# Decay factors of the gated delta rule from broadcast rows of cumulated sums, and two gate tiles moved from the plain to the block product

## The chip, the cores and the metric

The kernel runs on one core of a Trainium2 chip. The metric is the device time of one execution in microseconds (us), the median over several executions. The engines are TensorE (PE in the profile, its weight loads PEld), VectorE (DVE), ScalarE (ACT), GpSimd (POOL) and SyncE (SP), each with an instruction queue of its own that is worked off in order.

## What is computed

One decoder layer on 1024 tokens of width 1024: an input projection, two token mixers side by side (a gated delta rule with 8 heads of 128, and latent attention), their merge through sigmoid gates, a layer norm, a feed-forward block and a second layer norm. The change touches the delta rule's preparation and the gates' projection. For each head, with chunks of tokens, the reference does this:

```python
g = jnp.cumsum(g, axis=-1)                                # log decays, summed within the chunk
diff = g[..., :, None] - g[..., None, :]
decay = jnp.where(tril, jnp.exp(jnp.where(tril, diff, 0.0)), 0.0)
l_mat = jnp.where(strict, jnp.einsum('bnhid,bnhjd->bnhij', k_beta, k) * decay, 0.0)
intra = jnp.where(tril, jnp.einsum('bnhid,bnhjd->bnhij', q, k) * decay, 0.0)
q_dec = q * jnp.exp(g)[..., None]
...
o_dn = rms_norm(o_dn, dn_norm_w[i]) * jax.nn.silu(z)      # z: 8 of the 24 gate tiles
mixed = jax.nn.sigmoid(gate_dn) * y_dn + jax.nn.sigmoid(gate_mla) * y_mla   # the other 16
```

The kernel works with chunks of 128 tokens, so a head has 8 of them.

## The kernel before

All products are made of two parts for each operand, a high and a low one: `split` casts the high part on ACT (line 63) and subtracts it from the source for the low part on DVE (line 64). Three matmuls (high-high, high-low, low-high) stand for each fp32 product.

The projection `x @ w_in` has 24 tiles of 128 columns for q, k, v (with a short convolution behind each) and 24 gate tiles (8 for z, 16 for the two gates). They are worked off in two ways. A **plain gate tile** (`gate_tile`, line 155) is 8 x 3 x 2 = 48 matmuls of 128x128 by 128x512 into two of the four PSUM banks A to D; three gate tiles run at the very start in another form, and with `NG0 = 6` the tiles 3, 4 and 5 are plain ones. A **pair** (`pair`, line 479) takes two tiles at once and forms their 2x2 block product with 7 products in place of 8, of 12 matmuls each (line 501), so 84 matmuls for two tiles. Four of the 7 products need sums of x quarters: T1, T2, T3 and T4, which DVE (lines 450, 451) and POOL (452, 453) form after the early phase out of a second load of x (line 445, tiles `c0` to `c3`, tags for each of the four rows of blocks k), and which are then split as well. The ACT half of these splits is kept behind the last activation of gate tile 3 on ACT (`issue_after(g3.ins)`). The first pair's matmuls are kept behind the last transposes of `rope_q` on PE. The products of all pairs use the banks A, B, C, D in turn, so a product can begin when the one four before it has been read. The first two pairs (`first`) do their three products with plain quarters of x first, then T2, T1, T3, T4.

The pairs stand in a list: four blocks of three convolution pairs and some gate pairs, by `NGB = (1, 1, 2, 5)`. That is 12 + 9 = 21 pairs. After the third pair of a block, four **units** of `dn_unit` become due (two heads, two halves of the sequence), and one of them is issued behind each of the next pairs; there are 16.

A unit loads q, k and v of a head and 512 tokens, transposes them (line 587 for k and q, 604 for v, PSUM tag `t` with two buffers), and forms the decays: 8 small scaled copies of a triangular mask on ACT (568), two fp32r matmuls with `m_gt_r` (572) and one bf16 matmul that adds -1e30 above the diagonal (573), an Exp out of PSUM into `dm` (575), two fp32r matmuls with ones (578) and an Exp out of PSUM into `er` (580). Then POOL multiplies `er` by k and q (609), PE forms k.k and k.q (616, PSUM tag `s` with two buffers, which the two decay results use too), and DVE scales these by `dm` (619).

The order of instructions on each engine is set by a planner that simulates a timeline when the program is built; the program text gives only dependences and hints.

Of the kernel before, what the change touches and what calls it, by code (L numbers as in the profile page):

```python
# [7 lines left out]
F32 = mybir.dt.float32  # L8
F32R = mybir.dt.float32r
BF16 = mybir.dt.bfloat16  # L10
I32 = mybir.dt.int32
AF = mybir.ActivationFunctionType
ALU = mybir.AluOpType
# [4 lines left out]
P = 128  # L18
S = 1024
D = 1024  # L20
NT = S // P
KT = D // P
H = 8
# [13 lines left out]
def tile_hybrid_block(ctx: ExitStack, tc: tile.TileContext, A: dict):  # L37
    nc = tc.nc
# [23 lines left out]
    def split(src, hi, lo):  # L62
        nc.scalar.copy(hi, src)  # L63
        nc.vector.tensor_tensor(lo, src, hi.bitcast(F32), ALU.subtract)  # L64

    dram = pool(ctx, "dram", space=DRAM)
# [6 lines left out]
    n_d = dram.tile([P, 64, 64], F32, name="n_d")  # L73
    u_d = dram.tile([P, 64, 64], F32, name="u_d")
    v11_d = dram.tile([64, 64, 64], F32, name="v11_d")
    z_d = dram.tile([H, P, S], F32, name="z_d")
    gdn_d = dram.tile([KT, P, S], F32, name="gdn_d")
    gml_d = dram.tile([KT, P, S], F32, name="gml_d")
# [16 lines left out]
    nhalf = high.tile([P, 4], F32, name="nhalf", padded_shape=[P, 56])  # L95
    const = pool(ctx, "const")
    masks = const.tile([P, 4, P], F32, name="masks")
    ident, m_gt, m_le, m_neg = (masks[:, i] for i in range(4))
    m_gt_r = const.tile([P, P], F32R, name="m_gt_r")
    ident_b = const.tile([P, P], BF16, name="ident_b")  # L100
    neg_b = const.tile([P, P], BF16, name="neg_b")
    ones = const.tile([P, P], F32, name="ones")
    nc.vector.memset(ones, 1.0)
    ones_r = const.tile([P, P], F32R, name="ones_r")
    nc.scalar.copy(ones_r, ones)
    half = const.tile([P, 64], F32, name="half")
    nc.vector.memset(half, 0.5)
    nc.vector.memset(nhalf, -0.5)
# [3 lines left out]
    sk = const.tile([P, H, NT], F32, name="sk")  # L112
    ck = const.tile([P, H, NT], F32, name="ck")
    beta = const.tile([P, NT, H], F32, name="beta")
    eg = const.tile([P, NT, H], F32, name="eg")
    egd = const.tile([P, NT, H], F32, name="egd")
    egl = const.tile([P, NT, H], F32, name="egl")
    g_hl = const.tile([P, 2, NT, H], F32R, name="g_hl")

    xs = ExitStack()  # L120
    xp = pool(xs, "xp", side="right")
# [13 lines left out]
    def s_tile(tag="s"):  # L135
        return psf.tile([P, 512], F32, name=tag, bufs=2)
# [36 lines left out]
    pp = pool(p1, "p1")  # L173
# [8 lines left out]
    for k in range(KT):  # L182
# [12 lines left out]
            nc.sync.dma_start(out=xst[:, ns], in_=A["xT"][:, k, ns])  # L195
        if k == 2:
            nc.scalar.dma_start(out=masks, in_=A["masks"])
            nc.scalar.copy(m_gt_r, m_gt)
            nc.vector.tensor_copy(ident_b, ident)
            nc.vector.tensor_copy(neg_b, m_neg)  # L200
            nc.scalar.dma_start(out=cw, in_=A["conv_w"])
            nc.scalar.dma_start(out=dnw, in_=A["dn_norm_w"])
# [7 lines left out]
        for m in range(NF):  # L210
            for j, (a, b) in enumerate(HL):
                for n in range(2):
                    nc.tensor.matmul(fps[m][n], fw[m][k // 4][a][:, k % 4], xT[b][k][n],
                                     start=(k == 0 and j == 0), stop=(k == KT - 1 and j == 2))
    NG0 = 6


    def lat_w(off, wd):
# [100 lines left out]
    def side():  # L319
# [18 lines left out]
        for hf in range(2):  # L338
            tp = s_tile("t").rearrange("p (t a) -> p t a", t=4)
# [26 lines left out]
        nc.scalar.activation(nea, alog[:, 0], AF.Exp)  # L366
        g = pp.tile([P, NT, H], F32, name="g")
        nc.vector.scalar_tensor_tensor(g, acc, -1.0, nea.unsqueeze(1).broadcast_to([P, NT, H]), op0=ALU.mult, op1=ALU.mult)
        split(g, g_hl[:, 0], g_hl[:, 1])
        yield  # L370
        yield
        gc = s_tile()[:, 0:P].rearrange("p (a t h) -> p a t h", a=2, t=NT)
        nc.tensor.matmul(gc[:, 0], m_le, g, start=True, stop=True)
        nc.tensor.matmul(gc[:, 1], ones, g, start=True, stop=True)
        nc.scalar.activation(eg, gc[:, 0], AF.Exp)
        nc.scalar.activation(egl, gc[:, 1], AF.Exp)
        gcs = pp.tile([P, NT, H], F32, name="gcs")
        nc.vector.tensor_copy(gcs, gc[:, 0])
        nc.vector.tensor_tensor(gcs, gc[:, 1], gcs, ALU.subtract)
        nc.scalar.activation(egd, gcs, AF.Exp)  # L380


    def rope_q(t, cq):
# [42 lines left out]
    def r_tile(tag, shape, dt=F32):  # L426
        return rp_.tile(shape, dt, name=tag, bufs=1)
# [131 lines left out]
    def dn_unit(h, hf):  # L559
        t0, ns = hf * 4, slice(hf * 512, (hf + 1) * 512)  # L560
# [1 line left out]
        kq = r_tile("c0", [P, 2, 512]) if hf == 0 else g2.tile([P, 2, 512], F32, name="kq", bufs=1)  # L562
        nc.sync.dma_start(out=kq[:, 0], in_=qkv_d[1][h][:, ns])
        nc.sync.dma_start(out=kq[:, 1], in_=qkv_d[0][h][:, ns])
        gm = r_tile("c2", [P, 2, 4, P], F32R)
        for i in range(2):
            for t in range(4):
                nc.scalar.activation(gm[:, i, t], m_le, AF.Copy, scale=g_hl[:, i, t0 + t, h:h + 1].bitcast(F32))

        dps = s_tile().rearrange("p (t a) -> p t a", t=4)  # L570
        for i in range(2):
            nc.tensor.matmul(dps, m_gt_r, gm[:, i], start=i == 0, stop=False)
        nc.tensor.matmul(dps, neg_b, ident_b.unsqueeze(1).broadcast_to([P, 4, P]), start=False, stop=True)
        dm = r_tile("e4", [P, 4, P])
        nc.scalar.activation(dm, dps, AF.Exp)
        eps_ = s_tile().rearrange("p (t a) -> p t a", t=4)
        for i in range(2):
            nc.tensor.matmul(eps_, ones_r, gm[:, i], start=i == 0, stop=i == 1)
        er = r_tile("e5", [P, 4, P])
        nc.scalar.activation(er, eps_, AF.Exp)  # L580
        vT = r_tile("e0", [P, 512])
        nc.sync.dma_start(out=vT, in_=qkv_d[2][h][:, ns])
        ktok, vp = r_tile("e1", [P, 4, P]), r_tile("e2", [P, 4, P])
        for which in (0, 1):
            tp = s_tile("t").rearrange("p (t a) -> p t a", t=4)
# [16 lines left out]
        tp = s_tile("t").rearrange("p (t a) -> p t a", t=4)  # L602
# [24 lines left out]

    gates = [(24 + m, 24 + m + 1) for m in range(NG0, 24, 2)]
    dn_units = []
    NGB = (1, 1, 2, 5)  # L630
    order = []
    for b, ng in enumerate(NGB):
        h = 2 * b
# [516 lines left out]
    for t in range(NT):  # L1150
# [13 lines left out]
        for hf in range(2):  # L1164
            tp = s_tile("t").rearrange("p (h a) -> p h a", h=4)
# [51 lines left out]
    for q in range(4):  # L1217
# [7 lines left out]
        for t in range(NT):  # L1225
            tq = slice(t % 4 * P, (t % 4 + 1) * P)
            ps = s_tile()[:, 0:256]
            for k in range(KT):
                for j, (a, b) in enumerate(HL):
                    nc.tensor.matmul(ps, mT[a][k // 4, t // 4][:, k % 4, tq], wg[k][b], start=(k == 0 and j == 0),  # L1230
                                     stop=(k == KT - 1 and j == 2))
# [362 lines left out]
```

## Time and profile before

| | |
|---|---|
| time, three executions | 2102.81 us, 3379.37 us, 2095.53 us (median 2102.81) |
| the profiled execution | 2099.7 us, of which 2096.8 us from the first to the last instruction |
| TensorE clock granted, mean | 0.991 of full speed |
| busy share of the span | PE 97%, DVE 67%, ACT 45%, POOL 31% |

The execution that the profile was taken from lies between the two ordinary times of the table. A busy PE in the profile is one with a matmul under way; matmuls overlap, so a row's time is longer than the step from one matmul's start to the next.

### The profile page before, as it was taken

How to read it: one execution, taken by the hardware profiler on the slowest of the kernel's cores; microseconds unless marked ns; L12 is line 12 of the kernel's file. 1: busy time of each engine (PE TensorE's matmuls, PEld its weight loads, DVE VectorE, ACT ScalarE, POOL GpSimd, SP SyncE). 2: the span in 40 equal slices, each digit the busy share in tenths (PEclk: the TensorE clock that was granted, in tenths of full speed). 3: DMA queues.
4: the chain of work that ended last, by engine and by line, in shares of the span. 5: the costliest groups of instructions: out<-in, count | busy, mean ns of one | idle time of the engine just before them, and what ended most of it. 6: DMA issues, size and time to landing. Idle time of an engine off the chain costs nothing. (4 is left out here: it accounts for less than half of the span.)

```text
span 2096.8 us, 29713 instructions
## 1 busy us (share of the span) xinstructions
PE 2030.8 (97%) x10438; PEld 1710.7 (82%) x10438; DVE 1400.7 (67%) x2169; ACT 947.8 (45%) x1938; POOL 651.8 (31%) x567
## 2 busy tenths in 40 slices
PE   8999999999999999998999999999999999999998
PEld 7887887878787888787788788899888888887876
DVE  5548887877665655543556466487888788775576
ACT  5335576677574555444334233233333333343233
POOL 0115353434343998931111000100111121111942
PEclk9999999999999999999999999999999999999999
DMA  6344366555467212137977675025434344168773
GB/s 222 114 161 151 128 194 191 184 187 169 149 203 271 73 65 68 52 111 235 282 246 242 224 241 187 26 96 200 132 115 138 130 143 133 71 208 277 271 232 112
DMA packets 232661, 347.72 MB, mean 166 GB/s; under 512 B 44800, under 2 KB 123584, under 8 KB 231744
## 3 DMA queue, kind: packets, MB, share of 16 engines
q1 hardware_dynamic: 213184, 316.45, 46.0%
q10 hardware_dynamic: 15648, 13.65, 2.1%
q0 software_dynamic: 3680, 15.73, 2.1%
q8 instruction: 82, 1.34, 0.3%
q14 instruction: 67, 0.55, 0.1%
HBM read 228.01 MB, written 117.74 MB: 165 GB/s over the span
## 5 line engine op out<-in xcount | busy, mean ns | idle before, releaser
L1460 PE MATMUL f<-wh,xh 128*128 128x512 f32 x792 | 183.7, 392 | 5.5 <-ACT xh L63 3.7
L1460 PEld LDWEIGHTS f<-wh,xh 128*128 128x128 f32 x792 | 149.2, 189 | 39.2 <-ACT xh L63 4.5
L63 ACT CAST w<-S 128x512 fp32r<-128x512 f32 x172 | 106.1, 618 | 137.5 <-PE D L1273 42.8
L1372 POOL TENSOR_TENSOR T<-act 128x512 f32<-128x512 f32 x22 | 32.2, 1463 | 398.2 <-issue 138.8
L64 DVE TENSOR_TENSOR w<-S,w 128x512 fp32r<-128x512 f32 x172 | 136.1, 791 | 9.9 <-ACT w L63 9.7
L1273 PE MATMUL A<-m,w 128*128 128x512 f32 x504 | 121.2, 389 | 0.0
L1273 PEld LDWEIGHTS A<-m,w 128*128 128x128 f32 x504 | 94.5, 188 | 19.6
L827 POOL TENSOR_TENSOR nl<-nl,itmp 128x486 f32<-128x486 f32 (+44 forms) x106 | 107.2, 1027 | 1.4
L898 PE MATMUL y<-om,w 128*128 128x512 f32 x384 | 99.4, 405 | 3.0 <-ACT w L63 2.5
L825 POOL TENSOR_TENSOR itmp<-nl 128x486 f32<-128x486 f32 (+44 forms) x106 | 93.2, 898 | 16.7 <-DMA nl<-n_d 12.2
L1113 POOL TENSOR_TENSOR lrs<-sm,nhalf 128x1 f32<-128x1 f32 x16 | 23.2, 1454 | 229.7 <-issue 135.6
L1146 PE MATMUL f<-wo,m 128*128 128x512 f32 x384 | 90.7, 392 | 0.2 <-DVE acc L1104 0.2
L63 ACT CAST w<-wst 128x512 fp32r<-128x512 f32 (+1 forms) x52 | 42.3, 816 | 106.3 <-DMA wst<-in_w_br_mla_dram 44.9
L64 DVE TENSOR_TENSOR w<-wst,w 128x512 fp32r<-128x512 f32 (+1 forms) x52 | 50.2, 967 | 59.9 <-ACT w L63 59.8
L898 PEld LDWEIGHTS y<-om,w 128*128 128x128 f32 x384 | 70.3, 191 | 18.1 <-ACT w L63 3.3
L1146 PEld LDWEIGHTS f<-wo,m 128*128 128x128 f32 x384 | 71.4, 188 | 15.1 <-DVE acc L1104 0.6
L64 DVE TENSOR_TENSOR pt<-t,pt 128x512 fp32r<-128x512 f32 (+1 forms) x96 | 52.1, 554 | 43.7 <-ACT pt L63 43.2
L763 PE MATMUL o<-pt,vv 128*128 128x512 f32 (+3 forms) x288 | 76.3, 367 | 3.6 <-ACT pt L63 1.4
L743 DVE TENSOR_REDUCE row<-f 128x1 f32<-128x128 f32 (+3 forms) x64 | 48.2, 753 | 41.0 <-PE f L741 40.4
L549 DVE SCALAR_TENSOR_TENSOR c<-zo,cw,c 128x1023 f32<-128x1023 f32 (+2 forms) x42 | 61.8, 1472 | 14.4 <-ACT c L547 14.3
L1230 PE MATMUL s<-r,m 128*128 128x256 f32 x576 | 69.7, 283 | 0.0
L1230 PEld LDWEIGHTS s<-r,m 128*128 128x128 f32 x576 | 69.4, 192 | 0.1
(490 smaller groups left out, 5349.6 us busy)
## 6 DMA issues: line engine op xcount, KB each, us to landing
acc<-in_w_ffn_in_dram SPq DMA_DIRECT2D x44, 512.0 KB, 4.0
xs_d<-xo SPq DMA_DIRECT2D x88, 256.0 KB, 2.5
xh<-xs_d SPq DMA_DIRECT2D x88, 256.0 KB, 3.5
wst<-in_w_main_dram SPq DMA_DIRECT2D x25, 512.0 KB, 4.4
a<-in_w_ffn_out_dram SPq DMA_DIRECT2D x44, 256.0 KB, 5.2
raw<-in_w_main_dram SPq DMA_DIRECT2D x20, 512.0 KB, 4.5
xs<-xf_d SPq DMA_DIRECT2D x33, 256.0 KB, 3.5
wst<-in_w_br_mla_dram SPq DMA_DIRECT2D x16, 512.0 KB, 4.5
```

The source lines that it names most:

```text
L63: nc.scalar.copy(hi, src)
L64: nc.vector.tensor_tensor(lo, src, hi.bitcast(F32), ALU.subtract)
L549: nc.vector.scalar_tensor_tensor(acc[:, d:], v[:, 0:S - d], cw[:, m, 3 - d:4 - d], acc[:, d:], op0=ALU.mult, op1=ALU.add)
L743: nc.vector.tensor_reduce(nm, ps[:, 0:nk], axis=AX.X, op=ALU.max, negate=True)
L763: nc.tensor.matmul(po[:, i0 * P:512], vv[kt][a][:, hh * P:(hh + 1) * P], hl[b][:, 0:w], start=(kt == 0 and j == 0), stop=(kt == last and j ...
L825: nc.gpsimd.tensor_tensor(tv, nl[:, k0:kn_, k:k + 1].broadcast_to([P, kn_ - k0, w]), nl[:, k:k + 1, k + 1:64].broadcast_to([P, kn_ - k0, w ...
L827: nc.gpsimd.tensor_tensor(nl[:, k0:kn_, k + 1:64], nl[:, k0:kn_, k + 1:64], tv, ALU.subtract)
L898: nc.tensor.matmul(ps, w[a][:, k], od[b][:, k, ns] if dn else om[k][b], start=(k == 0 and j == 0), stop=(k == KT - 1 and j == 2))
L1146: nc.tensor.matmul(ps[:, ns], mT[a][kh, t // 4][:, k % 4, t % 4 * P:(t % 4 + 1) * P], wo[k][b][:, ns], start=(k == 0 and j == 0), stop=(k ...
L1230: nc.tensor.matmul(ps, mT[a][k // 4, t // 4][:, k % 4, tq], wg[k][b], start=(k == 0 and j == 0), stop=(k == KT - 1 and j == 2))
L1273: nc.tensor.matmul(bank, w[a][:, k], x[b][:, k], start=(k == 0 and j == 0), stop=(k == 3 and j == 2))
L1460: nc.tensor.matmul(bk, x[a][:, t * P:(t + 1) * P], w[b], start=(k == 0 and j == 0), stop=(k == HH - 1 and j == 2))
```

## The change

Each unit no longer forms its decays on PE. `side` (early, once) now transposes the cumulated sums and writes them to DRAM as rows (`gc_d`, one row of 128 for each head and chunk) and keeps their negative per token (`ngc`). A unit loads four rows, spread over all 128 partitions, into `gr[:, 0]`; POOL adds the mask `m_up` (-1e30 where a decay must vanish, 0 elsewhere) into `gr[:, 1]`; four Exp with the per-partition bias `ngc` give `dm`, and one Exp of `gr[:, 0]` gives `er`. The five matmuls and the eight small copies go. And `NG0` falls from 6 to 4, with one gate pair more in the second block: plain are the first three tiles and tile 3, and the list of pairs has 22 entries.

```diff
@@ side()
-        split(g, g_hl[:, 0], g_hl[:, 1])
...
-        nc.scalar.activation(eg, gc[:, 0], AF.Exp)
         nc.scalar.activation(egl, gc[:, 1], AF.Exp)
-        gcs = pp.tile([P, NT, H], F32, name="gcs")
-        nc.vector.tensor_copy(gcs, gc[:, 0])
-        nc.vector.tensor_tensor(gcs, gc[:, 1], gcs, ALU.subtract)
-        nc.scalar.activation(egd, gcs, AF.Exp)
+        gcs = pp.tile([P, H, NT], F32, name="gcs")
+        nc.vector.tensor_copy(gcs, gc[:, 0].rearrange("p t h -> p h t"))
+        nc.vector.tensor_scalar(ngc, gc[:, 0], -1.0, None, op0=ALU.mult)
+        gl = pp.tile([P, NT, H], F32, name="gl")
+        nc.vector.tensor_tensor(gl, gc[:, 1], ngc, ALU.add)
+        nc.scalar.activation(egd, gl, AF.Exp)
+
+        tp = s_tile("t")
+        nc.tensor.transpose(tp[0:H * NT, 0:P], gcs.rearrange("p h t -> p (h t)"), ident)
+        gr = pp.tile([P, P], F32, name="gr")
+        nc.scalar.copy(gr[0:H * NT], tp[0:H * NT, 0:P])
+        nc.scalar.dma_start(out=gc_d, in_=gr[0:H * NT])
@@ dn_unit()
-        gm = r_tile("c2", [P, 2, 4, P], F32R)
-        for i in range(2):
-            for t in range(4):
-                nc.scalar.activation(gm[:, i, t], m_le, AF.Copy, scale=g_hl[:, i, t0 + t, h:h + 1].bitcast(F32))
-
-        dps = s_tile().rearrange("p (t a) -> p t a", t=4)
-        for i in range(2):
-            nc.tensor.matmul(dps, m_gt_r, gm[:, i], start=i == 0, stop=False)
-        nc.tensor.matmul(dps, neg_b, ident_b.unsqueeze(1).broadcast_to([P, 4, P]), start=False, stop=True)
+        gr = r_tile("c2", [P, 2, 4, P])
+        nc.sync.dma_start(out=gr[:, 0].rearrange("p t a -> p (t a)"),
+                          in_=gc_d[h * NT + t0:h * NT + t0 + 4].rearrange("i p -> (i p)").partition_broadcast(P))
+
+        nc.gpsimd.tensor_tensor(gr[:, 1], gr[:, 0], m_up.unsqueeze(1).broadcast_to([P, 4, P]), ALU.add)
         dm = r_tile("e4", [P, 4, P])
-        nc.scalar.activation(dm, dps, AF.Exp)
-        eps_ = s_tile().rearrange("p (t a) -> p t a", t=4)
-        for i in range(2):
-            nc.tensor.matmul(eps_, ones_r, gm[:, i], start=i == 0, stop=i == 1)
+        for t in range(4):
+            nc.scalar.activation(dm[:, t], gr[:, 1, t], AF.Exp, bias=ngc[:, t0 + t, h:h + 1])
         er = r_tile("e5", [P, 4, P])
-        nc.scalar.activation(er, eps_, AF.Exp)
+        nc.scalar.activation(er, gr[:, 0], AF.Exp)
@@ lists
-    NG0 = 6
+    NG0 = 4
-    NGB = (1, 1, 2, 5)
+    NGB = (1, 2, 2, 5)
```

## Rows read from the trace of the kernel before

**Rows 1.** Page, part 1: busy time, share of the span, instructions of each engine.
```profile
PE 2030.8 (97%) x10438; PEld 1710.7 (82%) x10438; DVE 1400.7 (67%) x2169; ACT 947.8 (45%) x1938; POOL 651.8 (31%) x567
```

**Rows 2.** Windows, pair by pair: length, busy time, clock granted, DMA share, GB/s.
```profile
300.98:324.30 23.32, 23.32 (x111) 19.28 (x109) 21.06 (x28) 16.58 (x34) 10.69 (x7) 1.00 0.60 182
347.62:375.27 27.65, 25.49 (x110) 20.27 (x109) 15.97 (x29) 19.02 (x37) 9.10 (x7) 0.94 0.59 185
```

**Rows 3.** Waits of 250 to 650 us: us in total, times, longest.
```profile
PE s L616 <- ACT e L580: 5.5, 3, 2.0
...
PE s L616 <- ACT e L575: 2.4, 3, 2.0
```

**Rows 4.** Timeline of PE, a unit behind a gate pair; idle before in brackets.
```profile
569.38 1.93 PE L616 MATMUL s<-c 128*128 128x256 f32 x4 [2.01 <-ACT e L575]
...
573.66 2.08 PE L616 MATMUL s<-c 128*128 128x256 f32 x4 [1.49 <-ACT e L580]
...
579.80 0.61 PE L604 MATMUL t<-masks,e 128*128 128x128 f32 x4
```

**Rows 5.** Timeline of ACT at the same unit.
```profile
567.44 1.28 ACT L575 ACT_TABLE_LOAD   x1
...
571.72 1.28 ACT L580 ACT_TABLE_LOAD   x1
...
573.51 2.14 ACT L568 ACTIVATE c<-masks,g_hl 128x128 fp32r<-128x128 f32 x7
...
576.02 0.59 ACT L591 ACTIVATE e<-t 128x512 f32<-128x512 f32 x1
```

**Rows 6.** Timeline of PE at one unit's decays: start, us, instructions.
```profile
277.66 0.61 PE L572 MATMUL s<-c,m_gt_r 128*128 128x512 f32 x2
...
278.80 1.03 PE L587 MATMUL t<-masks,kq 128*128 128x128 f32 x8
```

**Rows 7.** Window of PE alone: busy, clock granted, DMA share, GB/s.
```profile
560.00:580.00 20.00, 16.50 (x59) 0.74 0.39 131
```

**Rows 8.** DMA issues: count, KB each, us to landing.
```profile
gm<-rv_d SPq DMA_DIRECT2D x16, 256.0 KB, 5.2
```

**Rows 9.** Timeline of POOL beside the x sums.
```profile
159.47 1.29 POOL L474 TENSOR_TENSOR S<-S,wst 128x512 f32<-128x512 f32 x1
```

**Rows 10.** Timeline of PE, two products of a pair.
```profile
200.82 2.88 PE L501 MATMUL A<-xT,w 128*128 128x512 f32 x12
203.54 2.88 PE L501 MATMUL B<-xT,w 128*128 128x512 f32 x12
```

**Rows 11.** Timeline of PE where the first pair begins.
```profile
165.18 5.73 PE L161 MATMUL C<-xT,w 128*128 128x512 f32 x24 [2.17 <-ACT zo L166]
...
184.35 0.61 PE L501 MATMUL D<-T,w 128*128 128x512 f32 x2
...
190.72 0.73 PE L501 MATMUL D<-T,w 128*128 128x512 f32 x2 [0.47 <-DVE T L64]
```

**Rows 12.** Timeline of DVE: last rope split, first and last x sum.
```profile
142.60 0.69 DVE L64 TENSOR_TENSOR stk<-qro,stk 128x512 fp32r<-128x512 f32 x1 [0.74 <-ACT stk L63]
...
159.56 1.74 DVE L450 TENSOR_TENSOR e<-c 128x512 f32<-128x512 f32 x1 [6.27 <-DMA c<-in_xT_dram]
...
164.59 0.68 DVE L64 TENSOR_TENSOR w<-wst,w 128x512 fp32r<-128x512 f32 x1
...
189.27 1.40 DVE L64 TENSOR_TENSOR T<-e,T 128x512 fp32r<-128x512 f32 x1
```

**Rows 13.** Timeline of ACT, the end of gate tile 3.
```profile
165.98 0.62 ACT L166 ACTIVATE zo<-D 128x512 f32<-128x512 f32 x1
```

**Rows 14.** Timeline of SP at the load of x.
```profile
153.70 19.73 SPq L445 DMA_DIRECT2D c<-in_xT_dram  x8
```

**Rows 15.** SP's own waits, 100 to 210 us: total, times, longest.
```profile
SPq L487 <- DVE w L64: 23.5, 1, 23.5
```

**Rows 16.** Window of all engines while the x sums are made.
```profile
178.00:191.00 13.00, 12.20 (x50) 8.77 (x49) 13.00 (x14) 9.17 (x21) 8.02 (x6) 1.00 0.22 82
```

More of the change, by code (lines that the diff above doesn't have):

```diff
@@ L75, in tile_hybrid_block @@
     v11_d = dram.tile([64, 64, 64], F32, name="v11_d")
+    gc_d = dram.tile([H * NT, P], F32, name="gc_d")
     z_d = dram.tile([H, P, S], F32, name="z_d")
@@ L97, in tile_hybrid_block @@
     masks = const.tile([P, 4, P], F32, name="masks")
-    ident, m_gt, m_le, m_neg = (masks[:, i] for i in range(4))
-    m_gt_r = const.tile([P, P], F32R, name="m_gt_r")
+    ident, m_up, m_le, m_neg = (masks[:, i] for i in range(4))
     ident_b = const.tile([P, P], BF16, name="ident_b")
@@ L103, in tile_hybrid_block @@
     nc.vector.memset(ones, 1.0)
-    ones_r = const.tile([P, P], F32R, name="ones_r")
-    nc.scalar.copy(ones_r, ones)
     half = const.tile([P, 64], F32, name="half")
@@ L114, in tile_hybrid_block @@
     beta = const.tile([P, NT, H], F32, name="beta")
-    eg = const.tile([P, NT, H], F32, name="eg")
+    ngc = const.tile([P, NT, H], F32, name="ngc")
     egd = const.tile([P, NT, H], F32, name="egd")
     egl = const.tile([P, NT, H], F32, name="egl")
-    g_hl = const.tile([P, 2, NT, H], F32R, name="g_hl")
     xs = ExitStack()
@@ L197, in tile_hybrid_block @@
             nc.scalar.dma_start(out=masks, in_=A["masks"])
-            nc.scalar.copy(m_gt_r, m_gt)
+            nc.vector.tensor_scalar(m_up, m_up, -1e30, None, op0=ALU.mult)
             nc.vector.tensor_copy(ident_b, ident)
```

## The prediction

> **What bounds the kernel now.** I read the page's first part, then windows cut at the pairs, then the timelines of each engine inside one pair, and last the waits. PE is busy for 97% of the span, DVE for 67% [rows 1]. The reader should not stop at the average: the change lies in two stages, the start of the block products (140 to 191 us) and the stage of pairs with units (250 to 630 us). In a convolution pair with a unit behind it, PE is busy for all of 23.32 us, DVE for 21.06, ACT for 16.58, POOL for 10.69 [rows 2]. So PE sets the pace there and what leaves PE's queue leaves the span, but DVE stands only 2.3 us behind. In a gate pair with a unit the same length is 27.65 us with 25.49 busy and a clock of 0.94 [rows 2]: there PE waits. The waits of 250 to 650 us say for what: line 616 (k.k and k.q) waits 5.5 and 2.4 us for the two Exp of the decays [rows 3], because the results that these read occupy both buffers of the tag `s` that line 616 needs. One such place shows waits of 2.01 and 1.49 us on PE [rows 4], and ACT beside it loading a table for each of the two Exp [rows 5], since the planner put a gate's activation between them.
>
> **The decays in the units.** Removed are five matmuls of a unit. From the first of them to the next work on PE is 277.66 to 278.80, so 1.14 us [rows 6]; times 16 units that is 18.2 us. The first unit's five ran while PE stood before the first T2 product, so I count 15 units: 17.1 us. All of it is on PE, in stretches where PE has no idle time, hence on the path. This is the firm term.
>
> The waits of line 616 are 7.9 us together [rows 3]; the buffers that they wait for are no longer written by the decays, so this wait in its present form is gone. What is late next: ACT is late there for another reason, its gate activations and table loads, and these stay. The square of k (line 591), which frees a transpose buffer for v's transposes at line 604, ends at 576.6 [rows 5], and PE came to line 604 at 579.80 [rows 4]. Without the 3.5 us of waits, and at full clock, PE is there several microseconds earlier, before ACT is; ACT's seven small copies ahead of it (2.14 us) go, four Exp instead of one come. So a part of the wait moves from 616 to 604. Bounds 0 and 7.9 us gained; I take 3, nearer to the rows of 604 than to the sum.
>
> The clock: the stretches with these waits show 0.94 over 27.65 us [rows 2] and 0.74 over 20 us [rows 7], so 1.7 and 5.2 us of full-speed work lost, 6.9 together. Bounds 0 and 6.9; I take 3, in step with the waits.
>
> Added to a unit: a load of 256 KB, one add on POOL, four small Exp. A broadcast of the same shape elsewhere in the kernel takes 5.2 us to land [rows 8]; it is issued with the unit's other loads on SP, ahead of v's load and of the stores, and it waits for `c2`, last read by the Exp of the unit before, some 20 us earlier, so nothing behind it on SP is held. DMA share is 0.60 in such a pair [rows 2]. Small copies cost ACT 2.14 us for seven [rows 5], 0.31 each: eight go (2.4 us), and four Exp of that size in place of one large one come (about 0.6 us more), an estimate by the same row. ACT gets lighter by some 1.8 us. POOL gets one add of 128x512; its add of that size took 1.29 us [rows 9] in 10.69 busy of 23.32. Behind it in POOL's queue stand the products with `er` and the weight sums of the pair; POOL's wait for the new row delays these only if the row is late. All three I cost at nothing; the cover is the slack of ACT and POOL just named. If it fails, DVE waits for `dm`, and with it the weight splits that PE needs: that is the first rival.
>
> Units together: 17.1 + 3 + 3 = 23 us less, bounds 17.1 and 31.9.
>
> **The two gate tiles.** Counted in matmuls, the move gains 96 - 84 = 12. One product of 12 takes 203.54 - 200.82 = 2.72 us [rows 10], so plain tiles cost 21.8 us, the pair 19.0, and the move would be worth 2.7 us less. But the two kinds stand at different places. Tiles 4 and 5 fill PE while DVE, POOL and ACT make the sums of x. The first T2 product begins at 184.35 and stands twice for its operands, the last time until 190.72 [rows 11]; the last low part was written at 189.27 + 1.40 = 190.67 [rows 12]. PE met this chain almost exactly. Take 21.8 us of cover away, and PE has gate tile 3 and three products to do (10.9 + 8.2 us), then waits for T2, since the fourth bank belongs to it and all later products come behind. So the 19.0 us of the new pair are paid in full, and what comes back is only by how much T2 is ready earlier.
>
> When is that? The ACT half of the T splits is held behind gate tile 3's last activation, 165.98 + 0.62 = 166.60 now [rows 13]; from there T2 took 24.1 us more. Tile 3 uses banks C and D, which the last rope transposes need first; their last operand is done at 142.60 + 0.69 [rows 12]. Without tile 4 between them the transposes and two casts (estimated at 0.6 us each, as ACT's square of that size in rows 5) can end at about 145.5, tile 3's matmuls 10.9 us later, and its activations 2 to 3.6 us after that (3.6 is what they took now: the matmuls ended at 165.18 - 2.17 = 163.0 [rows 11]). That makes 158.5 to 160, or up to 165.4 if the planner lets the first pair's products on A and B (5.4 us) go first. The chain behind it can shrink: the eight loads of x are issued over 19.73 us from 153.70 on [rows 14], behind a load for which SP waited 23.5 us, until the weight split of tile 5 gave a buffer free [rows 15]. Without tiles 4 and 5 that wait has no reason; two of four blocks, half of the 19.73 us, may be in and summed before the splits may start. So T2 takes between 24.1 - 9.9 = 14.2 and 24.1 us from there. Ready then at 172.7 to 189.5 against 190.67: a gain of 1.2 to 18 us. I take 9, near the middle, as no row is nearer to either end.
>
> The hole that this opens in PE, some 10 to 20 us, can cost clock. After idle times of 2.01 and 1.49 us close together a window fell to 0.74 [rows 4, 7]. Bounds 0 and 5.2 us, the loss in that window; I take 2. The Trainium skill ("TensorE: Matmul & The Clock Gate", section "Why this matters for your kernels") asks for no long idle gap between bursts of matmuls, since the clock falls back to 1.2 GHz after one; by that rule this hole does cost clock, which speaks against moving the two tiles. The fall to 0.74 agrees with it.
>
> `side` gets a transpose, a copy, a store and small DVE operations in place of others, well under 1 us, on the early path; no term.
>
> **Sum.** 2099.7 (the profiled execution; 2.9 of it outside the span) - 23 + 19 - 9 + 2 = 2088.7, rounded to 2089. The median of the runs, 2102.81, and the other ordinary run, 2095.53, lie around the profiled one; 0.35% separates them. Bounds: 2099.7 - 31.9 + 19 - 18 = 2068.8 and 2099.7 - 17.1 + 19 - 1.2 + 5.2 = 2105.6.
>
> **Rivals.**
> First, DVE becomes the bound. A DVE subtract of 128x512 took 0.68 us alone and one 1.74 beside a POOL add of 1.29 [rows 9, 12]: about 1.1 us lost for each POOL operation that meets it. One more POOL add a unit brings DVE to 22.1 in a pair whose PE work has shrunk to 22.2. Weight splits and bank reads then come late, and the 1.14 us do not arrive in the 7 or 8 convolution pairs with a unit (8 to 9 us given up), and the 3 us of waits reappear elsewhere: 2097 to 2103. Against it: gate pairs, with 16 us of DVE work in 27, take up arrears. The Trainium skill ("SBUF — State Buffer", section "Who interferes with whom") says that a DVE operation with two SBUF inputs and a GpSimd operation that reads SBUF exclude each other for the whole instruction; the trace agrees, with 1.74 against 0.68 us.
> Second, and slower: the hole before the first T2 product stays as long as the cover that was removed. If T2 is ready no earlier than 189.5, if the clock falls in the hole, and the waits in the units move to line 604 whole, the sum is the upper bound, 2105.6, up to 2112 where the sums come later still because the first pair's own weight splits now compete with them. It decides from the point where T2 is ready after about 187 with the units at their lower bound. For it: DVE was busy without a break from 178 to 191 [rows 16]. Against it: SP's wait of 23.5 us falls away.
> Third, the hole hardly opens, because sums can be made in the idle time before tile 3, and waits and clock come back whole: 2099.7 - 31.9 - 2.7 = 2065.1.
> That the change does not do what it says would need Exp table loads to multiply until ACT is the bound, at 1.28 us each [rows 5]; with 16.58 of 23.32 us busy I give it nothing of its own.
>
> **How the numbers follow.** Forecast 0.60 (its own range 2075 to 2099), DVE bound 0.16, the long hole 0.13, the full gain 0.11. The range 2066 to 2110 takes in the bounds and leaves out the ends of the second and third rival, and a different order by the planner elsewhere. 2% is 42 us, about what a measurement of this kernel can tell from no change; the four times lie within it; beyond it are the outer ends of the third case (0.06, faster) and of the second (0.06, slower), should the planner's order elsewhere add to them; 0.88 within.
>
> **What would show it.** In the profile after: PE without lines 572, 573 and 578, cycles of convolution pairs near 22.2 us; no wait at 616, some at 604; the first T2 product ready between 173 and 190 us with an idle PE of 10 us or more before it; one more set of seven products in the 200 to 650 us stage. The end of the pairs should come some 11 us earlier. Wrong would be: DVE busy throughout the pairs with PE waiting for weight splits, or a start of the pairs that is no earlier than now.

## The result, and the profile after

The changed kernel takes 2124.05 us (median; 2118.0 to 2128.81), the kernel before beside it 2104.07 us: ratio 1.0117, 95% interval 1.0101 to 1.0133. By the ratio it is slower by some 25 us, within the 2%; the two medians stand closer because one of the four executions of before took 3379.37 us. The median of after is 14 us above the upper end of the range. Its profiled execution took 2128.81 us, with a span of 2127.0 us.

I cut both traces at the same two places: where the tenth product of the first two pairs begins on PE (nine are then done), and where the first projection behind the pairs begins. Windows of the three stretches, first of before, then of after; columns as in [rows 16]:

```profile
140.00:203.54 63.54, 60.57 (x271) 48.62 (x269) 45.83 (x52) 31.61 (x58) 28.65 (x19) 1.00 0.42 146
203.54:662.14 458.60, 450.75 (x2054) 369.55 (x2052) 351.18 (x496) 295.49 (x578) 182.92 (x134) 0.99 0.56 178
662.14:2096.80 1434.66, 1391.55 (x7415) 1177.24 (x7413) 924.46 (x1413) 559.60 (x1148) 426.41 (x390) 0.99 0.49 162
```

```profile
140.00:203.52 63.52, 50.58 (x181) 37.99 (x180) 40.42 (x50) 27.51 (x47) 29.95 (x22) 0.81 0.39 142
203.52:683.97 480.45, 456.75 (x2062) 373.59 (x2061) 364.55 (x511) 266.23 (x505) 215.23 (x152) 0.98 0.58 183
683.97:2127.00 1443.03, 1392.80 (x7415) 1175.37 (x7413) 918.53 (x1413) 560.18 (x1148) 426.31 (x390) 0.99 0.48 161
```

The start gives nothing: 181 matmuls on PE in place of 271, the same 63.5 us. The pairs take 21.9 us more: PE is busy 6.0 us longer and idle 15.9 us longer (23.7 against 7.9). The part behind the pairs, whose code the change does not touch and where PE has the same 7415 matmuls in the records, takes 8.4 us more. Together 30.2 us between these two executions; the one of after is the slowest of its four.

**In the pairs.** PE's waits of 250 to 650 us, against [rows 3] (a unit's lines stand 3 lower in after: 601 is 604 of before, 613 is 616; those of a pair and of the x sums stand 3 higher: 504 is 501, 448 is 445):

```profile
PE t L601 <- ACT e L588: 15.1, 6, 4.4
PE t L601 <- DMA e<-dv_d: 2.6, 1, 2.6
```

The 7.9 us at k.k and k.q are gone, as forecast, and 17.7 us stand at the transposes of v, which in six of seven places wait for the square of k on ACT to free a buffer of `t`. The longest of the six, on ACT, DVE, POOL, SP and PE in turn:

```profile
294.01 1.28 ACT L575 ACTIVATE e<-c,ngc 128x128 f32<-128x128 f32 x4
...
300.89 0.63 ACT L577 ACTIVATE e<-c 128x512 f32<-128x512 f32 x1 [3.51 <-DMA c<-gc_d]
...
303.63 1.28 ACT L553 ACT_TABLE_LOAD   x1 [1.07 <-DVE c L552]
304.92 1.06 ACT L553 ACTIVATE c<-c 128x1024 f32<-128x1024 f32 x1
...
311.73 1.15 ACT L550 ACTIVATE c<-pre,cw 128x1024 f32<-128x1024 f32 x1 [5.24 <-DMA dq_d<-c]
...
313.29 0.58 ACT L586 COPY e<-t 128x512 f32<-128x512 f32 x1
313.77 0.60 ACT L588 ACTIVATE e<-t 128x512 f32<-128x512 f32 x1
```

```profile
301.84 1.71 DVE L552 SCALAR_TENSOR_TENSOR c<-zo,cw,c 128x1021 f32<-128x1021 f32 x1
```

```profile
300.94 1.53 POOL L572 TENSOR_TENSOR c<-c,masks 128x512 f32<-128x512 f32 x1 [1.31 <-DMA c<-gc_d]
302.43 3.95 POOL L606 TENSOR_TENSOR e<-e,kq 128x512 f32<-128x512 f32 x2
```

```profile
296.19 0.56 SPq L569 DMA_DIRECT2D c<-gc_d  x1
...
306.41 0.38 SPq L607 DMA_DIRECT2D qe_d<-e  x1
306.88 0.46 SPq L554 DMA_DIRECT2D dq_d<-c  x1
```

```profile
314.42 1.12 PE L601 MATMUL t<-masks,e 128*128 128x128 f32 x4 [4.38 <-ACT e L588]
```

Read it backwards. PE stood 4.38 us for a square that ACT made at 313.77. Ahead of it on ACT the convolution's copy had waited 5.24 us for the store of its own buffer `c3`. That store went out at 306.88, after a Silu that ended at 305.98. ACT had stood 3.51 us at `er`'s Exp for the row before that, but this wait was over: the Silu's table load last waited 1.07 us for the last tap of the convolution on DVE, which ended at 303.55, and DVE had no idle time from 296.37 on. What the row can have added here is at most the 0.9 us between 305.98 and 306.88, in which the store stood on SP behind that of `qe_d`, whose data POOL, late for the row too, finished at 306.38. The row was requested at 296.19, right after the four Exp of the unit before (294.01 + 1.28) had freed `c2`. My "some 20 us earlier" for that buffer was wrong: the planner keeps the Exp of `dm` until shortly before DVE needs them.

**At the start.** SP, DVE, PE and ACT of after, against [rows 14], [rows 12], [rows 11] and [rows 13]; the first row is one of SP's own waits of 100 to 180 us, against [rows 15]:

```profile
SPq L490 <- POOL S L477: 23.5, 1, 23.5
```

```profile
156.24 0.33 SPq L490 DMA_DIRECT2D wst<-in_w_main_dram  x1
156.66 10.54 SPq L448 DMA_DIRECT2D c<-in_xT_dram  x6
```

```profile
146.78 0.69 DVE L64 TENSOR_TENSOR stk<-qro,stk 128x512 fp32r<-128x512 f32 x1 [0.74 <-ACT stk L63]
```

```profile
149.21 4.43 PE L504 MATMUL A<-xT,w 128*128 128x512 f32 x12
153.47 2.90 PE L504 MATMUL B<-xT,w 128*128 128x512 f32 x12
156.21 1.29 PE L158 MATMUL C<-xT,w 128*128 128x512 f32 x5
...
193.22 1.22 PE L504 MATMUL D<-T,w 128*128 128x512 f32 x2 [0.95 <-DVE T L64]
```

```profile
170.29 0.61 ACT L163 ACTIVATE zo<-D 128x512 f32<-128x512 f32 x1
```

The wait of 23.5 us on SP did not go with tiles 4 and 5. The loads of x now stand behind the third pair's weights, whose buffer is held by a sum on POOL, and go out at 156.66, 3 us later than before. The planner put the first pair's two products ahead of gate tile 3, whose last activation ends at 170.90 in place of 166.60. T2 is complete at 193.2 us and not 9 us earlier; before, profiled three times with this start (before, b0 and b1 below), has it between 190.7 and 193.7 us, so it has not moved. The granted clock over 140 to 200 us is 0.83, 0.83 and 0.75 in windows of 20 us, behind idle times of PE of 3.16 and 2.28 us: PE's idle time did cost clock. The Trainium skill ("TensorE: Matmul & The Clock Gate", section "Why this matters for your kernels"), which warns of long idle gaps between bursts of matmuls, agrees with the clock of these rows. How much of the lost clock is hidden, since T2 and not PE ends this stretch, is not shown: the T splits are held behind gate tile 3, and the product on A just ahead of it took 153.47 - 149.21 = 4.26 us where it takes 2.72 at full clock [rows 10], so up to 1.5 us of the price may stand in T2's time.

### The profile page after: what moved, and what is told of

Its sections match the earlier page's. It is cut to its first block, busy times and chain, and to the rows that moved or that the text cites. A ratio compares the mean times of both kernels' runs of the same rounds, so it can differ in the third digit from the quotient of the medians.

```text
span 2127.0 us, 29530 instructions
## 1 busy us (share of the span) xinstructions
PE 2028.3 (95%) x10347; PEld 1702.9 (80%) x10347; DVE 1401.0 (66%) x2180; ACT 912.7 (43%) x1850; POOL 684.8 (32%) x587
## 5 line engine op out<-in xcount | busy, mean ns | idle before, releaser
L1143 PEld LDWEIGHTS f<-wo,m 128*128 128x128 f32 x384 | 71.4, 188 | 15.1 <-DVE acc L1101 0.6
L504 PE MATMUL C<-xT,w 128*128 128x512 f32 x276 | 72.2, 407 | 3.7 <-ACT zo L163 2.7
```

The costliest lines, as they stand in the source:

```text
L504: nc.tensor.matmul(bk, w[a][:, k], x[b][k], start=(k == 0 and j == 0), stop=(k == 3 and j == 2))
L1143: nc.tensor.matmul(ps[:, ns], mT[a][kh, t // 4][:, k % 4, t % 4 * P:(t % 4 + 1) * P], wo[k][b][:, ns], start=(k == 0 and j == 0), stop=(k ...
```

## Experiments

All runs below after are compared with the kernel before on the same chip (2097 to 2098 us). "Start", "pairs" and "behind" are the three stretches above, of the profiled execution; idle is the length of the pairs less PE's busy time. A profiled execution can lie off the median: those of u2 (2139.4 us) and u3 (2118.2) are the slowest of theirs. The expectations of v1, v2 and v12 count one pair too many: the list has 21 before, 22 after, 20 with eight plain tiles, so "21", "22", "23" and "odd" there read 20, 21, 22 and even; the differences of one are right.

| kernel | median us | ratio, interval | start | pairs (idle) | behind |
|---|---|---|---|---|---|
| before (profile) | | | 203.5 | 458.6 (7.9) | 1434.7 |
| after (profile) | 2124.05 | 1.0117 [1.0101, 1.0133] | 203.5 | 480.5 (23.7) | 1443.0 |
| u1_decays_only | 2107.46 | 1.0042 [1.0027, 1.0056] | 209.1 | 461.1 (22.6) | 1434.7 |
| u2_gates_only | 2132.51 | 1.0164 [1.0143, 1.0184] | 198.5 | 489.0 (16.9) | 1450.1 |
| u3_kcopy_dve | 2112.81 | 1.0074 [1.0045, 1.0102] | 203.7 | 468.8 (16.3) | 1443.9 |
| v2_decays_kcopy | 2093.64 | 0.9981 [0.9965, 0.9997] | 207.8 | 449.6 (16.3) | 1434.0 |
| b1_before_kcopy | 2103.21 | 1.0026 [1.0015, 1.0038] | 205.5 | 462.8 (12.6) | 1429.8 |
| v6_no_row | 2135.35 | 1.0186 [1.0162, 1.0210] | 202.3 | 487.6 (30.3) | 1445.8 |
| v10_er_late | 2131.56 | 1.0157 [1.0135, 1.0179] | 202.2 | 485.3 (27.7) | 1443.5 |
| v12_ng6_kcopy_er | 2108.77 | 1.0051 [1.0032, 1.0069] | 207.3 | 464.7 (25.9) | 1436.7 |
| u4_x_act | 2124.35 | 1.0129 [1.0107, 1.0152] | 199.9 | 478.8 (22.8) | 1443.8 |
| v3_x_first | 2121.71 | 1.0121 [1.0104, 1.0138] | 200.5 | 481.7 (22.6) | 1441.1 |
| v4_x_first_nohold | 2120.58 | 1.0111 [1.0090, 1.0131] | 196.4 | 483.2 (23.8) | 1441.1 |
| v1_ng8 | 2139.06 | 1.0196 [1.0177, 1.0215] | 224.0 | 462.1 (27.6) | 1450.5 |
| w1_bank_shift | 2117.17 | 1.0088 [1.0065, 1.0110] | 198.9 | 469.4 (16.2) | 1443.6 |
| w2_pair_at_end | 2107.11 | 1.0039 [1.0023, 1.0055] | 200.2 | 461.8 (11.6) | 1442.5 |
| b0_before_again | 2105.39 | one run | 206.6 | 460.5 (10.4) | 1436.2 |
| w3_odd_end | 2101.20 | 1.0013 [0.9998, 1.0027] | 197.6 | 466.0 (15.3) | 1433.9 |
| w4_odd_end_x_nohold | 2107.17 | 1.0044 [1.0028, 1.0059] | 195.5 | 465.4 (14.6) | 1448.7 |

### Each part alone

```diff
# u1_decays_only, against after
-    NG0 = 4
+    NG0 = 6
-    NGB = (1, 2, 2, 5)
+    NGB = (1, 1, 2, 5)
# u2_gates_only: the opposite edit, made in before
```

> The decays from rows, with gate tiles 4 and 5 plain as before (21 pairs). Theory A (the two parts add: the extra pair costs its 19 us in full, the decays save 17 us on TensorE and lose about as much to waits at v's transposes, line 601, and to clock): within 6 us of the kernel before, so 2098 to 2110 us where before is 2104, with 10 to 20 us of waits at line 601. Rival R1 (the new row load and GpSimd add are the loss, the extra pair is free): 2118 to 2126 us. Rival R2 (the waits at 601 come only from the shifted order of pairs): 2080 to 2090 us.

> The decays as before, gate tiles 4 and 5 moved into a 22nd pair. Theory A: 19 us for seven more products, and nothing back at the start because the first T2 product is ready no earlier: 2119 to 2128 us where before is 2104, the first T2 product ready at 190 to 195 us, line 616 still waiting for its two Exp. Rival R1: 2100 to 2108 us. The forecast's own price of this part was +12 us: 2116.

Both parts lose alone, 9 and 34 us by the ratios, where together they lose 25: the parts do not add. u1 came within its range, though not within 6 us of the kernel beside it; u2 is 4.5 us beyond the range of its theory A, and far from its rival. The decays alone take 12.3 us of busy time out of the pairs (438.5 against 450.8) and put 14.7 us of idle time in: the waits at the transposes of v are 17.4 us, ten times. The stage of pairs is so only 2.5 us longer; the start is 5.6 us longer in this profile, 3 us of which are within what before itself shows (203.5 to 206.6). The gates alone put 21.4 us of busy time in, where I said 19.0, keep the waits at line 616 (12.1 us in place of 7.9) and take 15.4 us more behind the pairs. In this profile the start is 5 us earlier.

### ScalarE's queue at the transposes

```diff
# u3_kcopy_dve against after; v2_decays_kcopy against u1; b1_before_kcopy against before
-                nc.scalar.copy(ktok, tp)
+                nc.vector.tensor_copy(ktok, tp)
-                nc.scalar.activation(sq, tp, AF.Square)
+                nc.scalar.activation(sq, ktok, AF.Square)
```

> The changed kernel with k's transposes copied out by VectorE and squared from that copy, so that the transpose buffer no longer waits for ScalarE. Theory A (the waits at line 601, 15.1 us, and most of 8 us of clock in the pairs come from ScalarE's queue holding that buffer): 2101 to 2112 us where the changed kernel has 2124, waits at 601 under 4 us. Rival R3 (TensorE waits for late data in general, DVE as well): the waits move to DVE's weight splits or to 601 for DVE, 2118 to 2126 us.

> The new decays alone (six plain gate tiles, 22 pairs), with the copy of k in the units on DVE and the square made from that copy. Theory A (ScalarE's queue is late at the transposes of v, and each operation taken from ahead of the square counts): the copy gave back 11 us where four plain tiles stood, so 2107.5 - 11 = 2096 us, the waits at the transposes of v about 7 us instead of 17.4, the stage of pairs 450 us instead of 461. Rival (ScalarE stands for the row that is loaded, and what it does behind that wait is no matter): 2104 to 2108 us, waits of 14 us or more.

> The kernel before, unchanged but for the copy of k in the units, which goes to DVE, with the square made from that copy: a control for the new decays with the same copy (2093.6 us, ratio 0.998). Theory A (in the kernel before PE waits for the two large Exp of the decays and not for the copy, so the copy gives nothing there, and the new decays with it are worth what separates the two): 2096 to 2103 us, waits at the products of k of 5 to 9 us. Rival (a lighter ScalarE is the whole of it, and the removed matmuls bring nothing): 2089 to 2094 us, waits there of 3 us or less.

One copy per unit, off the queue that is late, and the buffer of the transposes is freed by DVE. The wait in u3 (250 to 650 us), and windows of the pairs of v2 and then of b1:

```profile
PE t L601 <- DVE e L586: 7.2, 6, 1.6
```

```profile
207.76:657.38 449.62, 433.36 (x1977) 353.61 (x1976) 347.22 (x511) 254.87 (x480) 205.61 (x148) 1.00 0.60 192
```

```profile
205.50:668.31 462.81, 450.23 (x2054) 369.60 (x2052) 365.92 (x512) 287.72 (x562) 180.34 (x134) 0.99 0.56 177
```

15.1 us of waits became 7.2 (all waits at the transposes of k and v: 17.7 and 12.3), and by the ratios the kernel is 9 us faster, 13 us with six plain tiles. u3's waits did not fall under the 4 us expected, and half of them moved to DVE, as its rival had it; its time misses the 2112 us of theory A by 0.8. v2 came in at 2093.6 where 2096 was said; it is the one version faster than before, by 4 us, and narrowly (interval 0.9965 to 0.9997). The control shows that the copy alone brings before nothing (1.0026, if anything slower), with 12.3 us of waits at the products of k, more than the 5 to 9 expected. So with the copy of k on DVE in both, the new decays are worth 0.45%, 9 us, and PE's busy time in the pairs falls by 450.2 - 433.4 = 16.9 us.

### Is it the row?

```diff
# v6_no_row, against after: the row is not loaded; the masks' tile stands in
-        nc.sync.dma_start(out=gr[:, 0]..., in_=gc_d[...].partition_broadcast(P))
-        nc.gpsimd.tensor_tensor(gr[:, 1], gr[:, 0], m_up..., ALU.add)
+        nc.gpsimd.tensor_tensor(gr[:, 1], masks, m_up..., ALU.add)
-            nc.scalar.activation(dm[:, t], gr[:, 1, t], AF.Exp, bias=ngc[...])
+            nc.scalar.activation(dm[:, t], gr[:, 1, t], AF.Exp, bias=nhalf[...])
-        nc.scalar.activation(er, gr[:, 0], AF.Exp)
+        nc.scalar.activation(er, masks, AF.Exp)
# v10_er_late against after, v12_ng6_kcopy_er against v2: er's Exp behind the square of k
+                sqi = nc.scalar.activation(sq, tp, AF.Square)
+                with tc.issue_after(sqi.ins):
+                    nc.scalar.activation(er, gr[:, 0], AF.Exp)
```

> The kernel after without the load of the row in the units: the masks' tile stands in for it, so the decays are computed from other numbers, with the same instructions on POOL and ScalarE. Theory A (the row is loaded late, ScalarE and POOL stand for it 45 and 39 us, and all that stands behind them is late at the transposes of v): the waits there fall from 17.7 us to 5 us or less, the stage of pairs from 480 to 466 us, the whole to 2108 to 2112 us. Rival (ScalarE is late through its gate activations, table loads and the copies of the convolution; the row's wait lies in time that it has to spare): the waits stay at 13 us or more, the whole 2119 to 2125 us.

> The kernel after, with the unit's Exp of the plain row placed behind the square of k on ScalarE; nothing else. Theory A (ScalarE stands 3 to 6 us at this Exp, first for the row and, without the row's load, for the store of the unit before, and the copy and square of k stand behind it): waits at the transposes of v fall from 17.7 us to 5 to 9 us, the stage of pairs from 480 to 468 to 473 us, the whole 2112 to 2117 us. Rival (of the six waits only one has this Exp as the stall ahead of it, the others the convolution's copy, which waits for its own store, and its Silu, which waits for DVE): 14 us or more stay, the whole 2120 to 2126 us.

> The new decays with six plain gate tiles and 22 pairs, the copy of k on DVE, and the Exp of the plain row behind the square of k on ScalarE. Theory A: the Exp's wait no longer stands ahead of the squares, the 10 us that PE still waited at the transposes of k and v with the copy alone fall to 6 us or less: 2087 to 2091 us. Rival (with the copy on DVE the transposes' buffers no longer wait for ScalarE's queue, so the Exp's place is no matter): 2092 to 2096 us.

ScalarE stood 44.9 us for the row in after, 13 times. Without the load (250 to 650 us, PE and then ACT; line 598 is 601 of after, 574 its 577):

```profile
PE t L598 <- ACT e L585: 15.9, 7, 4.1
...
ACT e L574 <- DMA qe_d<-e: 13.6, 5, 5.2
```

The waits of PE stay whole. The same Exp now stands for the store of the unit before, out of the buffer that it writes. Removing this wait uncovered the next one at the same place, so nothing here supports the theory that the late row is the loss. It is not a clean test: the kernel is slower than after as a whole, 2135.4 us, since the planner also ordered the pairs and what follows anew. With the Exp behind the square, PE's waits at the transposes of v fall only to 12.7 us, and others open (v10, then v12, PE and ACT, 250 to 650 us):

```profile
PE t L602 <- ACT e L586: 10.7, 6, 3.8
PE B L504 <- DVE zo L508: 3.2, 1, 3.2
PE B L504 <- ACT w L63: 2.7, 2, 2.2
...
ACT L575 <- DVE c L617: 14.4, 7, 3.6
```

```profile
PE C L504 <- ACT w L63: 10.1, 3, 3.5
PE D L504 <- ACT w L63: 5.7, 2, 3.5
...
ACT L575 <- DVE c L617: 22.5, 8, 3.6
```

Moved back, the unit's Exp push a table load, which waits for DVE's last use of the old `dm` (22.5 us, 8 times, in v12), and the new `dm` in front of weight splits, which PE's products need: 15 us slower in v12 than in v2. Both runs miss their theory and the time of their rival: 2131.6 and 2108.8 us. What the three runs leave standing is narrower than a late row: ScalarE works in order, several different waits stand ahead of the square, and what helped is to take the release of the buffer off that engine. In after, of the six places the stall just ahead is the convolution's copy three times (6.1 us of PE's waits), its Silu (4.65 us for DVE, at 476 and 594) twice (7.8 us), and the Exp that waits for the row once (1.3 us).

### The start

```diff
# u4_x_act, against after
-            nc.sync.dma_start(out=v, in_=A["xT"][:, r * 4 + k])
+            (nc.scalar if k < 2 else nc.sync).dma_start(out=v, in_=A["xT"][:, r * 4 + k])
# v3_x_first, against after: xl keeps the loads of x
+            with tc.issue_after(xl[3].ins) if npair[0] == 3 else nullcontext():
                 nc.sync.dma_start(out=st, in_=A["w_main"][m])
# v4_x_first_nohold: v3, and
-            with tc.issue_after(g3.ins):
-                split(v, *[xq[nm][i][k] for i in range(2)])
+            split(v, *[xq[nm][i][k] for i in range(2)])
```

> The changed kernel with the second load of x (blocks k = 0 and 1, four loads) issued from ScalarE's queue and not from SP's, where it stands behind a weight load that waits 23.5 us. Theory A for the start (SP's order keeps the x sums late): x sums begin before 150 us in place of 160.9, the first T2 product ready 4 to 12 us earlier, 2112 to 2120 us. Rival R4 (the split of the sums is held by gate tile 3's last activation, at 170.9 us, whatever x does): T2 within 3 us of 193, 2121 to 2127 us.

> The kernel after with the third pair's weight loads placed behind the fourth load of x on SP, so that the first loads of x do not stand behind a load that waits 23.5 us for a buffer. Theory A (this wait sets when the sums of x are made, and so the T2 tiles): loads of x issued before 145 us instead of from 156.7 us, T2 ready 8 to 15 us earlier than 193 us, the tenth product begun at 190 to 196 us instead of 203.5 us, the whole 2111 to 2118 us. Rival (the ScalarE half of the T splits is held behind the last activation of gate tile 3, at 170.9 us, and takes its time from there): T2 ready within 3 us of 193 us, the whole 2121 to 2127 us.

> The kernel after with the third pair's weight loads behind the fourth load of x, as in the run where four loads of x were out by 142 us and T2 was still only ready at 193 us, and without the hold of the ScalarE half of the T splits behind the last activation of gate tile 3. Theory A (that hold is what T2 counted from: 171 us and 22 us of sums and splits behind it): T2 ready at 178 to 185 us, the tenth product begun at 188 to 194 us instead of 200.5 us, the whole 2110 to 2116 us. Rival (the four blocks of sums go at the pace of DVE, POOL and the second four loads of x, 5.8 us a block): T2 ready at 189 us or later, the whole 2119 to 2124 us.

On ScalarE's queue (u4) the loads only went out at 155.0 us, behind a weight split that waited for PE, so this run did not bring x earlier; T2 came at 191.2 us and the time in the range of its rival. In v3 four of them went out early, and the last part of T2's product still began at 193 us, 0.3 us sooner (first SP, then PE of v3; the third row is PE of v4):

```profile
132.11 10.31 SPq L448 DMA_DIRECT2D c<-in_xT_dram  x4
```

```profile
192.96 0.73 PE L505 MATMUL D<-T,w 128*128 128x512 f32 x2 [0.80 <-DVE T L64]
```

```profile
188.78 0.84 PE L504 MATMUL D<-T,w 128*128 128x512 f32 x3
```

So SP's wait was not what T2 counted from. Without the hold it is ready 4 us sooner, between the two expectations, and the start is 7 us earlier than in after. What is left is the work of DVE and POOL on the sums: DVE's operations of 128x512 take 0.68 us alone there and up to 1.79 beside POOL's, as in [rows 9, 12]. What the whole kernel keeps of the 7 us is not clear of the spread (ratios 1.0111 and 1.0117, with overlapping intervals); the pairs behind are 2.7 us longer. v4's time is the one that its rival gave.

### Behind the pairs

```diff
# v1_ng8, against before
+    NG0 = 8;  NGB = (1, 1, 2, 4)
# w1_bank_shift: u3, and
+    npair, nbank = [0], [1]
# w2_pair_at_end: u3, and
+    NGB = (1, 1, 2, 6)
# w3_odd_end: w2, and (w4: w3 with the edits of v4)
+    npair, nbank = [1], [0]
```

> The kernel before with eight plain gate tiles and 21 pairs (the old decays stay): the gate tiles moved the other way. Counted in products: two plain tiles more (+21.8 us at the start), one pair less (-19.0 us in the pairs), so 2.7 us slower. Theory A (the number of pairs sets the order that the planner gives the scan stage behind the pairs; 22 pairs twice gave 1434.7 us behind the pairs, 23 pairs 1443 to 1450): an odd number again, so the part behind the pairs is 1442 to 1451 us, and the whole 2109 to 2116 us. Theory B (fewer plain tiles make that part longer, through what is left over from the start): with more plain tiles it is 1434 us or less, and the whole 2098 to 2102 us. For the start both say 220 to 225 us until the tenth product of the first pairs has begun, against 203.5 us.

> The kernel after with the copy of k on DVE (2112.8 us; 1443.9 us behind the pairs) and the accumulator banks of the pairs counted from the second one on, which changes the planner's order in the scan stage and no instruction there. Theory A (the order behind the pairs sets that part's time): it differs from 1443.9 us by more than 3 us, to either side, between 1434 and 1451 us. Rival (the number of pairs itself, by what is left over from them): 1442 to 1446 us. The start changes too, since gate tile 3 then meets other banks; I give it no number.

> The kernel after with the copy of k on DVE, and the added gate pair placed in the last group (1, 1, 2, 6) instead of the second: the order behind the pairs is the same on every engine. Theory A (order): 1443.9 us behind the pairs, within 1.5 us. Rival (spread from run to run, or where the pair stands): more than 3 us away from it. In the stage of pairs a gate pair without a unit beside it costs no more than its seven products, 19.0 us; one with a unit costs waits besides, so 2 to 6 us less than 468.8 us, the whole 2106 to 2111 us.

> The kernel before, word for word. Theory A (order): 1434.7 us behind the pairs within 2 us, 458.6 us for the pairs within 2 us. Rival (spread): 4 us or more off in one of the two.

> The kernel after with the copy of k on DVE, the added pair in the last group (2107.1 us; 1442.5 us behind the pairs), and the alternation of the pairs' buffers begun with the other set, so that the last pair has the set that it has in the kernel before. Theory A (that set is what makes the part behind the pairs longer): 1433 to 1437 us behind the pairs, the whole 2097 to 2102 us. Rival (the number of pairs in another way, or the order): 1441 to 1450 us, the whole 2104 to 2112 us.

> The same, with the two edits of the start beside it: the third pair's weight loads behind the fourth load of x, and no hold of the T splits (with both the tenth product began 7 us earlier in the kernel after). Theory A: 1433 to 1437 us behind the pairs, the start 194 to 198 us, the whole 2092 to 2098 us. Rival: 1441 to 1450 us behind the pairs, the whole 2100 to 2108 us.

First I thought of the number of pairs: one fewer (v1) gave 1450.5 us too. w3 ends that, with the added pair and 1433.9 us; w4 ends the other idea, the buffer set of the last pair, with the same set and 1448.7 us. Windows of the part behind the pairs, w3 and then w4:

```profile
663.67:2097.60 1433.93, 1393.93 (x7415) 1178.30 (x7413) 921.89 (x1413) 559.23 (x1148) 426.80 (x390) 0.99 0.49 162
```

```profile
660.85:2109.50 1448.65, 1398.64 (x7415) 1178.58 (x7413) 922.49 (x1413) 560.13 (x1148) 426.21 (x390) 0.99 0.48 160
```

What goes with the time is the order of the instructions there. The kernels that have the order of before on all five engines (before twice, u1, v2, v12, b1) took 1429.8 to 1436.7 us; those with the order of after (after, u3, u4, v3, w2) 1441.1 to 1443.9; the others, each with one of its own, 1433.9 to 1450.5, with w1 at after's time all the same, so that its expectation, which asked for a difference, missed. The 8.4 us of after lie from the first preparation of the scan to the output projection: 305 us (from 967) against 296 (from 946), with PE's idle time there 26.4 against 18.5 us. PE's waits in it, before and after:

```profile
PE y L898 <- ACT w L63: 3.9, 3, 2.0
...
PE o L1004 <- DVE on L1001: 2.0, 2, 1.8
```

```profile
PE y L895 <- ACT w L63: 6.8, 3, 5.0
PE o L1001 <- DVE on L998: 4.3, 2, 2.5
PE p L804 <- ACT po L807: 2.5, 1, 2.5
```

Which swap in the order does it was not isolated. In v1 the start came as expected (224.0), but the pairs gave none of the 19 us back: 11.6 us of one wait of PE for a mask copy of the decays, and 12.5 us at line 616. v1's whole, 2139.1 us, is beyond both of its expectations. w2 gave 2107.1 us, in its range: the place of the added pair was worth 7.0 us in the pairs.

## Why the prediction was wrong, by its steps

- **Five matmuls a unit, -17.1: right.** v2 against b1 gives 16.9 us of PE's busy time in the pairs. u1 against before gives 12.3, at a clock of 0.98 and not 0.99.
- **The waits of line 616, a gain of 3: wrong, and the first step that failed.** They went, as said, and waits at line 604 came, as said; but what "moves" was 17.7 us for 7.9, a loss of 9.8 in place of a gain of 3. I had bounded it by the rows of a place where ACT was only just ahead [rows 4, 5], and taken ACT as 1.8 us lighter. Its busy time did fall; its order and what it waits for decided. Both bounds of this term excluded a loss without a reason.
- **The added row, at nothing: wrong as argued, and not the whole cause.** `c2` is free only just before, POOL and ScalarE stand 39 and 45 us for the row; yet without it PE waits as long.
- **Clock, -3: wrong sign.** The counts ask for 19.0 - 17.1 = 1.9 us more of busy time in the pairs, 6.0 are there: some 4 us lost at a clock of 0.98.
- **The new pair, +19.0: right.** From u1 to after busy time rises by 456.8 - 438.5 = 18.3 us (from before to u2 by 21.4).
- **T2 ready 9 us earlier: wrong, the second step that failed.** "Without tiles 4 and 5 that wait has no reason" fell at once: another releaser, the same 23.5 us; and gate tile 3 came after the first two products, 5.5 us beyond the latest time that I gave it (170.9 for 165.4). Most of that is the last rope operand on DVE, which I had taken over from [rows 12] and which was done 4.2 us later (147.5 for 143.3; 2.3 us of this are there at the first rope transposes already, 101.6 for 99.3, where before profiled again has 102.1); the rest is about what the product on A lost at the lower clock. From there T2 took 22.3 us, near the upper of my bounds of 14.2 and 24.1.
- **Clock of the hole, +2: open.** The clock fell; what of it the stretch paid for was not isolated, 1.5 us at most by the product on A.
- **"A different order by the planner elsewhere" I left out of the range**: it was 8.4 us.

The second rival named the right side and, with T2 ready after 187 us, its point was reached. Its 2105.6 to 2112 us lacked the loss in the units and the 8.4 us behind the pairs. The first rival came true in a small part: DVE did not become the bound (364.6 us busy of 480.5), but PE's waits for weight splits, on DVE and ACT, were none before in 250 to 650 us and are 5.5 us after. The terms against the two executions: the units and the added pair, forecast at -4, are +21.9 in the pairs; the start, forecast at -7, is 0; the rest, forecast at 0, is +8.4. That the start came out at just 0 is partly luck, since two profiles of before differ by 3 us there.

## What to carry to other kernels

Work taken from the busiest engine is worth its busy time only if the in-order queue that feeds it is not late with the next buffer; look at what stands ahead of the releasing instruction on that queue, and move the release to an engine that is free (here one copy to DVE turned a loss of 9 us, u1, into a gain of 4, v2). A wait counted on some engine is no loss by itself: take its cause away before mending it, since the next one may stand in the same place. And where a planner orders a whole kernel, an edit can cost as much in a stage that it does not touch; cut both traces by stage before explaining the sum.

## What the runs showed of the hardware

A store holds its buffer until well after it is issued: that of `dq_d`, 512 KB, was issued at 306.88 us and the copy that overwrites the buffer began at 311.73, 4.85 us later. The spread load of four rows took 3.0 to 5.6 us to land, median 4.2, in the stage of pairs. The same program, profiled twice, gave 203.5 and 206.6 us for the start, 458.6 and 460.5 in the pairs and 1434.7 and 1436.2 behind them, where kernels with one and the same order lie up to 6.9 us apart (1429.8 and 1436.7); so differences of some 3 us between single profiles, and of up to 7 behind the pairs, say nothing here.
